# Straight stores of diagonal blocks, grouped norms, stores on another queue and two moved adds in a hybrid encoder layer

## The chip, the cores and the metric

One core of a Trainium2 chip runs the whole program. The metric is the device time of one execution in microseconds (us); less is better. The engines are TensorE (PE, matrix products; PEld is its weight load), VectorE (DVE), ScalarE (ACT), GpSimd (POOL) and SyncE (SP, which here only issues transfers). SP, ACT and GpSimd each have a queue of their own for issuing DMA transfers, and every engine and every queue works through its instructions in the order in which the program has them.

## The reference

One layer over 512 rows of width 2048, all in float32:

```python
h = rmsnorm(x, mix_norm)
proj = h @ w_mix_in
y_gdn = gdn_group(proj, ...)            # 8 heads of 128, gated delta rule
y_sc = shortconv_group(proj, sc_conv)   # gated short convolution, 1024 channels
x = x + concatenate([y_gdn, y_sc]) @ w_mix_out
x = x + memory_xattn(rmsnorm(x), rmsnorm(mem), w_q, w_k, w_v, w_o)   # 4 heads, 256 memory rows
x = x + conv_ffn(rmsnorm(x), w_up, conv_w, w_down)                   # SwiGLU, width 5632
return rmsnorm(x, final_norm)
```

In the delta-rule group, per head and chunk, with k normalised and `beta` and the decay from the projection:

```python
a_strict = where(strict, (k * beta) @ k.T * decay, 0)
sol = triangular_solve(eye + a_strict, [v * beta, k * beta * exp(g)], unit_diagonal=True)
attn = q @ k.T * decay
# over the chunks: v_new = u - w @ state; o = q' @ state + attn @ v_new; state = state * exp(g_last) + k'.T @ v_new
o = rmsnorm(o, out_gain) * silu(z)
```

## The kernel before, in words

**Products.** PE multiplies in a rounded float32 format, so every weight piece (128 x 1024, `wst`) is split in two: ACT casts the high part (`whi`, lines 146 and 516) and DVE subtracts for the low part (`wlo`, lines 147 and 517). A piece is multiplied by 8 products with `whi` over 512 columns and 8 with `wlo` over 256. `wst` has 5 buffers in the delta-rule stage, and SP issues the weights' loads.

**Order of work.** The memory's values come first (`values`, 28 pieces after the early ones; `beside_values(j)` puts other work ahead of piece j: loads of x, the sum of its squares in `xacc`, its norm, x's scaling). Then the folds of w_xv with w_xo, the input projection, the delta-rule stage, the rest of the attention, the FFN and the last norm. In blocks under `tc.manual_schedule` the named engines do their work in the order in which it is written; elsewhere a scheduler orders it.

**Pairs of projection blocks.** The input projection (20 pairs, `quads`) and the FFN's up-projection (44 pairs) multiply two neighbouring 2 x 2 block columns by seven products on sums of blocks. `quad_left` makes products 1, 2, 6 and 5, `quad_right` 7, 3 and 4. Products 1, 6, 7 and 4 share the accumulator `px`, 5 and 3 share `pz`: product 7 can't begin until `gb`, the copy of product 6, has been taken off `px`, nor product 3 until `ub`, the copy of product 5, has been taken off `pz`. For pair 0 the sums of blocks are made beforehand. In pair 1 the tiles `s1` and `s3` are made by two adds after product 2; later pairs get them by another way. `between[0]` to `between[3]` are calls put at set places of `quad_left`. In the FFN `run_held` takes up the unit held back from the pair before: norm of the gate half (`ug`), its convolution (`ucv`), Silu, the same for the up half (`uu`, without Silu), and their product `h`. For pair 1 the norm itself is ended in `between[0]` (`norm_rest`).

**Delta-rule stage.** PE goes through the products of w_xk (`psk`), w_xq (`pswk`) and the out projection in two rounds (`out_row`, `psx`; the second, for the delta rule's own heads, needs `yg`, read back from `y_d`). Chains of small work are woven into them by hand: `weave(chain, wait)` starts a generator, `place(cost)` and `tick` advance a clock by estimated PE time, and what a generator yields is PE's cost of the step and the time until its next one. For each half `hb` (4 heads) and chunk j:

- `prepare_chunk` loads decay, k and q, forms k's squared norms `ss`, the factors `bk` (1/ss times beta) and `nk` (its root, by Ln and Exp on ACT), and the matrix `nt` (128 x 128 for each of 4 heads). It then takes `nt`'s diagonal 32 x 32 blocks: a product with a mask into `nd`, a sum over the four blocks in a row into `ndc`, and a store to `nd_d`.
- `invert` reads the blocks of all four chunks back (`ab`), inverts them on DVE by 31 steps (`tm`, `xb`) and stores the inverses (`xd_d`).
- `solve` reads v and the inverses (`xd`), builds the inverse of the whole chunk (`pt`) and takes `nk`.
- `recur` goes over the chunks in order (`pv`, `vn`, `pso`, `pss`).
- `scaled` takes a result's sum of squares over the head on PE (`psn`), Ln and Exp on ACT, multiplies the result by it on DVE and by z on GpSimd, and stores it to `y_d`.

## Time and profile before

| | |
|---|---|
| median of 3 runs | 2705.7 us (2701.09 to 2709.1) |
| the profiled execution | 2705.68 us, span 2703.9 us, granted clock 0.996 |
| PE busy | 2657.2 us, 98% |
| DVE, ACT, POOL busy | 2261.4 us (84%), 1588.1 us (59%), 217.0 us (8%) |

The profile comes from one execution. A row of PE's waits gives what PE waited for, the total, the number of waits and the longest. A row of a timeline gives the start, the duration (for a group, from its first start to its last end), the engine, the line of the kernel, the operation, the tiles (output, arrow, inputs) and shapes; in brackets the engine's idle time ahead of it and what ended that. A row of a window gives its bounds and length, the busy time of PE, PEld, DVE, ACT and POOL with the number of instructions, then PEclk (the granted clock, 1 is full), the share of DMA time and GB/s. A row of a group of instructions gives minimum, median and maximum in ns, or busy time and mean. A row of DMA issues ends with KB and the median us from issue to landing.

Times by stage: values to about 106 us, first pair of the mixer at about 205 to 225, the delta-rule stage at about 750 to 1125, the FFN's first pairs at about 1400 to 1445.

### The profile page before, as it was taken

The numbers are of one execution on the slowest core, as the hardware profiler recorded it, in microseconds if no ns is written. First come the engines' busy times: TensorE is split into PE (matmuls) and PEld (weight loads), VectorE is DVE, ScalarE is ACT, GpSimd is POOL, SyncE is SP. The second block draws the span as 40 slices with busy tenths as digits, with TensorE's granted clock in tenths as the row PEclk, the third lists the DMA queues.
The fourth block names the chain that finished last, engine by engine and source line by source line (L and its number), as shares of the span: only waits on it lengthen the run. The fifth ranks groups of instructions, "written<-read, shape, count | busy, mean of one in ns | idle before, by whom it ended". The sixth has DMA issues, their size and how long they took to land.

```text
span 2703.9 us, 40155 instructions
## 1 busy us (share of the span) xinstructions
PE 2657.2 (98%) x14757; PEld 2292.9 (85%) x14757; DVE 2261.4 (84%) x3354; ACT 1588.1 (59%) x2305; POOL 217.0 (8%) x236
## 2 busy tenths in 40 slices
PE   9999999999998999999999999999999999999998
PEld 7878888888887897888888888888888888888886
DVE  7868788999999864456688999999999999877888
ACT  7675555666676565345675656565565655554545
POOL 0000000000100123000000000000000000000201
PEclk9999999999999999999999999999999999999999
DMA  8786766776676975665556676777767676864976
GB/s 298 234 259 183 183 162 174 189 199 183 186 222 204 312 226 174 229 199 189 172 171 165 177 192 174 197 182 180 191 178 202 167 198 204 257 189 141 285 248 183
DMA packets 265461, 544.69 MB, mean 201 GB/s; under 512 B 31776, under 2 KB 126640, under 8 KB 265264
## 3 DMA queue, kind: packets, MB, share of 16 engines
q1 hardware_dynamic: 192512, 400.53, 45.4%
q0 software_dynamic: 27920, 89.42, 19.2%
q10 hardware_dynamic: 44832, 52.18, 5.4%
q8 instruction: 115, 1.88, 0.3%
q14 instruction: 82, 0.67, 0.1%
HBM read 472.83 MB, written 67.39 MB: 200 GB/s over the span
## 4 chain that ended last, share of the span: by engine, by line
PE 87%; DVE 5%; DMA 4%; issue 2%; ACT 2%; SPq 0%; POOL 0%; ACTq 0%; DVEq 0%; POOLq 0%
PE px L172 19%; PE px L175 10%; PE pz L172 10%; PE pz L175 5%; PE py L172 5%; PE psd L1487 4%; PE psd L1485 4%; PE psd L1486 4%; PE psx L157 3%; PE psx L159 3%; PE psx L158 3%; PE py L175 2%; PE psk L172 2%; PE psk L1052 2%; PE pss L1145 1%
## 5 line engine op out<-in xcount | busy, mean ns | idle before, releaser
L172 PE MATMUL px<-xo,whi 128*128 128x512 f32 x2288 | 575.7, 394 | 6.7 <-ACT gb L598 5.2
L516 ACT CAST whi<-wst 128x1024 fp32r<-128x1024 f32 x290 | 304.8, 1051 | 343.5 <-PE pz L172 198.7
L172 PEld LDWEIGHTS px<-xo,whi 128*128 128x128 f32 x2288 | 412.8, 189 | 82.2 <-ACT gb L598 5.4
L517 DVE TENSOR_TENSOR wlo<-wst,whi 128x1024 fp32r<-128x1024 f32 x290 | 353.4, 1220 | 22.8 <-ACT whi L516 21.0
L175 PEld LDWEIGHTS px<-xo,wlo 128*128 128x128 f32 x2288 | 312.8, 191 | 22.4
L147 DVE TENSOR_TENSOR wlo<-wst,whi 128x1024 fp32r<-128x1024 f32 x204 | 255.4, 1254 | 90.1 <-ACT whi L146 87.9
L175 PE MATMUL px<-xo,wlo 128*128 128x256 f32 x2288 | 319.6, 283 | 0.0
L516 ACT CAST whi<-s 128x1024 fp32r<-128x1024 f32 x214 | 223.2, 1043 | 158.0 <-DVE wlo L517 83.8
L146 ACT CAST whi<-wst 128x1024 fp32r<-128x1024 f32 x204 | 213.6, 1049 | 165.0 <-issue 48.0
L172 PE MATMUL pz<-xo,whi 128*128 128x512 f32 x1152 | 289.0, 393 | 0.0
L517 DVE TENSOR_TENSOR wlo<-s,whi 128x1024 fp32r<-128x1024 f32 x214 | 261.1, 1221 | 0.2
L1487 PE MATMUL psd<-wlo,hdh 128*128 128x512 f32 x616 | 240.8, 391 | 2.9 <-DVE wlo L1281 2.8
L1485 PE MATMUL psd<-whi,hdh 128*128 128x512 f32 x616 | 240.0, 390 | 0.1
L1486 PE MATMUL psd<-whi,hdl 128*128 128x512 f32 x616 | 239.9, 389 | 0.0
L172 PEld LDWEIGHTS pz<-xo,whi 128*128 128x128 f32 x1152 | 207.2, 189 | 37.1 <-ACT whi L516 0.3
L1278 ACT CAST whi<-wst 128x1024 fp32r<-128x1024 f32 x99 | 104.3, 1053 | 122.6 <-issue 54.1
L175 PEld LDWEIGHTS pz<-xo,wlo 128*128 128x128 f32 x1152 | 157.2, 190 | 11.2
L175 PE MATMUL pz<-xo,wlo 128*128 128x256 f32 x1152 | 160.6, 282 | 0.0
L1487 PEld LDWEIGHTS psd<-wlo,hdh 128*128 128x128 f32 x616 | 115.6, 188 | 30.1 <-DVE wlo L1281 6.2
L172 PE MATMUL py<-xo,whi 128*128 128x512 f32 x560 | 140.2, 392 | 0.0
L1281 DVE TENSOR_TENSOR wlo<-wst,whi 128x1024 fp32r<-128x1024 f32 x99 | 121.2, 1224 | 20.5 <-ACT whi L1278 18.2
L1485 PEld LDWEIGHTS psd<-whi,hdh 128*128 128x128 f32 x616 | 115.6, 188 | 24.2 <-ACT whi L1278 0.4
(368 smaller groups left out, 5045.7 us busy)
## 6 DMA issues: line engine op xcount, KB each, us to landing
wst<-in_w_up SPq DMA_DIRECT2D x132, 512.0 KB, 4.0
wst<-in_w_dn SPq DMA_DIRECT2D x121, 512.0 KB, 4.5
s<-in_w_up POOLq DMA_DIRECT2D x87, 512.0 KB, 6.2
wst<-in_w_mix SPq DMA_DIRECT2D x84, 512.0 KB, 5.5
s<-in_w_mix POOLq DMA_DIRECT2D x55, 512.0 KB, 6.2
s<-in_w_up SPq DMA_DIRECT2D x43, 512.0 KB, 4.4
hid<-hf_d SPq DMA_DIRECT2D x77, 256.0 KB, 5.1
wst<-in_w_xo SPq DMA_DIRECT2D x32, 512.0 KB, 4.7
```

What stands on the lines that cost most here:

```text
L146: nc.scalar.copy(hi, st)
L147: nc.vector.tensor_tensor(lo, st, f(hi), op=ALU.subtract)
L157: nc.tensor.matmul(ps, wh, xh, start=first, stop=False)
L172: nc.tensor.matmul(ps, hi[:, k * P : (k + 1) * P], x, start=first and k == 0, stop=False, skip_group_check=True)
L175: nc.tensor.matmul(ps[:, n:], lo[:, k * P : (k + 1) * P], x[:, :n], start=False, stop=end, skip_group_check=True)
L516: nc.scalar.copy(hi, t)
L517: tt(lo, t, f(hi), op=ALU.subtract)
L1278: nc.scalar.copy(hi[:, i * n : (i + 1) * n], t)
L1281: tt(lo[:, sl], t, f(hi)[:, sl], op=ALU.subtract)
L1485: nc.tensor.matmul(ps, xh, wh, start=first, stop=False)
L1486: nc.tensor.matmul(ps, xl, wh, start=False, stop=False)
L1487: nc.tensor.matmul(ps, xh, wl, start=False, stop=last)
```

## The change

1. In `beside_values` the first norm of x begins at j 12 (was 10), ends at 14, x is scaled at 15 to 26 and the memory's norm taken at 27, each two pieces later.
2. In pair 1 of the mixer and of the FFN the two adds that make `s1` and `s3` are put on DVE behind the add to `ub` of the pair before (`behind`).
3. In the FFN's pair 1 `run_held` is called after `gb`'s copy and no longer ahead of product 6's split.
4. `prepare_chunk` stores the four diagonal blocks of `nt` by four transfers from GpSimd's queue, without the masked product, the sum and SP's store.
5. k's norms of the four chunks of a half lie in one tile of 16 columns; Ln and Exp are taken once for each half, in `invert`.
6. In `scaled` the results of chunks 0 and 1, and of 2 and 3, are finished together: z's load, the Exp and both multiplications of the even chunk wait for the odd one. The stores of `y_d`, and that of `xd_d` in `invert`, are issued by GpSimd.
7. The second half's `prepare_chunk` starts 75 clock units after the first half's (was 60), its `invert` 80 (was 65).

In each fence below, first the line of the kernel, then the operation, output, arrow, inputs, shape. ACT in the FFN's pair 1, from product 1's copy `ga` to product 5's copy `ub`, before:

```order
L577 COPY ga_14073<-px_14056 128x512
L516 CAST whi_14169<-s_2593_14044 128x1024
L516 CAST whi_14192<-wst_14050 128x1024
L1337 ACTIVATE ucv_14104<-ug_14101,cols 128x512
L516 CAST whi_14214<-wst_14048 128x1024
L1351 ACT_TABLE_LOAD
L1351 ACTIVATE ucv_14104<-ucv_14104 128x512
L1337 ACTIVATE ucv_14112<-uu_14109,cols 128x512
L598 COPY gb_14144<-px_14056 128x512
L603 COPY ub_14167<-pz_14146 128x512
```

and after:

```order
L577 COPY ga_14041<-px_14024 128x512
L516 CAST whi_14115<-s_2576_14069 128x1024
L516 CAST whi_14137<-s_2565_14012 128x1024
L534 ACTIVATE s_2603_14222<-wst_14216 128x1024
L516 CAST whi_14160<-wst_14018 128x1024
L599 COPY gb_14094<-px_14024 128x512
L1349 ACTIVATE ucv_14099<-ug_14096,cols 128x512
L516 CAST whi_14182<-wst_14016 128x1024
L1363 ACT_TABLE_LOAD
L1363 ACTIVATE ucv_14099<-ucv_14099 128x512
L1349 ACTIVATE ucv_14107<-uu_14104,cols 128x512
L604 COPY ub_14135<-pz_14114 128x512
```

`gb`'s copy now stands ahead of the held unit's convolution and table load; `ub`'s copy stays behind the whole of it.

DVE in the same place, from the splits of pair 1 to the norm's product `ug` (`rst`, `rsy` are the norm's last steps, `s_2643` a sum for pair 2), before:

```order
L517 TENSOR_TENSOR wlo_14125<-s_2610_14122,whi_14124 128x1024
L517 TENSOR_TENSOR wlo_14148<-s_2609_14119,whi_14147 128x1024
L238 TENSOR_TENSOR rst_13970<-rsy_13969 128x512
L593 TENSOR_TENSOR s_2643_14320<-s_2627_14245,wst_14248 128x1024
L239 SCALAR_TENSOR_TENSOR rst_13970<-rst_13970,ms_13967 128x512
L583 TENSOR_TENSOR ga_14073<-py_14079,ga_14073 128x512
L240 SCALAR_TENSOR_TENSOR rsy_13969<-rst_13970,rsy_13969 128x512
L565 TENSOR_TENSOR ga_14073<-ga_14073 128x256
L1346 TENSOR_TENSOR ug_14101<-ga_13908,rsy_13969 128x256
```

and after:

```order
L238 TENSOR_TENSOR rst_13938<-rsy_13937 128x512
L517 TENSOR_TENSOR wlo_14075<-s_2577_14072,whi_14074 128x1024
L239 SCALAR_TENSOR_TENSOR rst_13938<-rst_13938,ms_13935 128x512
L583 TENSOR_TENSOR ga_14041<-py_14047,ga_14041 128x512
L240 SCALAR_TENSOR_TENSOR rsy_13937<-rst_13938,rsy_13937 128x512
L565 TENSOR_TENSOR ga_14041<-ga_14041 128x256
L517 TENSOR_TENSOR wlo_14116<-s_2576_14069,whi_14115 128x1024
L1358 TENSOR_TENSOR ug_14096<-ga_13876,rsy_13937 128x256
```

The sum for pair 2 has left the place between the norm's steps, and the split of `s1` has come behind `ga`.

SP in the products of w_xq, where the second half's chunks are prepared, before:

```order
L884 DMA nd_d_79<-ndc_8665 128x4x32
L143 DMA wst_8906<-in_w_xq 128x1024
L143 DMA wst_8940<-in_w_xq 128x1024
L143 DMA wst_8984<-in_w_xq 128x1024
L143 DMA wst_9022<-in_w_xq 128x1024
L884 DMA nd_d_79<-ndc_8821 128x4x32
L910 DMA xd_d_80<-xb_8059 128x512
L143 DMA wst_9062<-in_w_xq 128x1024
L895 DMA ab_8840<-nd_d_79 128x1x512
```

and after:

```order
L143 DMA wst_9035<-in_w_xq 128x1024
L840 DMA v_8809<-qkvz_d 128x4x128
L925 DMA xd_8811<-xd_d_80 128x4x32
L143 DMA wst_9069<-in_w_xq 128x1024
L143 DMA wst_9109<-in_w_xq 128x1024
L840 DMA v_8920<-qkvz_d 128x4x128
L925 DMA xd_8922<-xd_d_80 128x4x32
L143 DMA wst_9182<-in_w_xq 128x1024
L900 DMA ab_8966<-nd_d_79 128x1x512
```

The stores of `ndc` and of the inverses have left SP's queue; the reads of `xd` and `ab`, which need GpSimd's stores, are still in it, with weights behind them.

The diff:

```diff
@@ -445,13 +445,13 @@
             squares(2 * j - 1)
         elif 8 < j < 16:
             mem_squares(j - 8)
-        if j == 10:
+        if j == 12:
             r0.append(norm_begin([xacc]))
-        elif j == 12:
+        elif j == 14:
             r0[0] = norm_end(r0[0])
-        elif j > 12 and j < 25:
-            norm_x(j - 13)
-        elif j == 25:
+        elif 14 < j < 27:
+            norm_x(j - 15)
+        elif j == 27:
             mem_cols()
 
     with tc.manual_schedule(engines={mybir.EngineType.PE, mybir.EngineType.SP, mybir.EngineType.Activation, mybir.EngineType.DVE}):
@@ -586,8 +586,9 @@
         if pos == 1:
 
             s1 = US("s1")
-            tt(s1, s3, a22, op=ALU.add)
-            tt(s3, s3, a11, op=ALU.subtract)
+            with tc.issue_after(behind[0].ins):
+                tt(s1, s3, a22, op=ALU.add)
+                tt(s3, s3, a11, op=ALU.subtract)
         if pos:
             s2 = US("s2")
             tt(s2, s1, a11, op=ALU.subtract)
@@ -604,11 +605,13 @@
         between[3]()
         return a12, a22, s2, s3, px, pz, ga, gb, ub
 
+    behind = []
+
     def quad_right(pos, left, whole):
 
         a12, a22, s2, s3, px, pz, ga, gb, ub = left
         product(px, wsplit(s3), 7, False)
-        tt(ub, px, ub, op=ALU.add)
+        behind[:] = [tt(ub, px, ub, op=ALU.add)]
         if not whole:
             together(ub)
         if pos:
@@ -830,7 +833,7 @@
             nc.tensor.transpose(v4(ps)[:, n], v4(t)[:, n], ident)
 
     kx, nt, at, bk, nk, pt, vv, ke, qd, qq = ({} for _ in range(10))
-    prepared, solved = [0, 0], {}
+    prepared, solved, sums = [0, 0], {}, {}
 
     def load4(s2, t, hb, j):
         d = T(s2)
@@ -855,7 +858,9 @@
         turn4(pst, k)
         four(psk, k, k)
         yield 1.4, 2.5, 0
-        ss = sp.tile([P, 4], F32, tag="ss", name=nm("ss"), bufs=3)
+        if j == 0:
+            sums[hb] = sp.tile([P, 16], F32, tag="ss", name=nm("ss"))
+        ss = sums[hb][:, 4 * j : 4 * j + 4]
         junk = T("junk")
         for n in range(4):
             nc.scalar.activation(v4(junk)[:, n], v4(pst)[:, n], AF.Square, accum_out=ss[:, n : n + 1])
@@ -866,9 +871,6 @@
         kx[i] = T("kx")
         nc.vector.tensor_tensor(v4(kx[i]), v4(pst), bc(kd[:, j, H4], P), op=ALU.mult)
         yield 0, 1.5, 0
-        nk[i] = sp.tile([P, 4], F32, tag="nk", name=nm("nk"), bufs=8)
-        nc.scalar.activation(nk[i], ss, AF.Ln, scale=0.25)
-        nc.scalar.activation(nk[i], nk[i], AF.Exp, scale=0.5)
         nt[i] = T("nt")
         for n in range(4):
             nc.vector.scalar_tensor_tensor(v4(nt[i])[:, n], v4(psk)[:, n], bk[i][:, n : n + 1], v4(dt)[:, n], op0=ALU.mult, op1=ALU.mult)
@@ -877,17 +879,20 @@
         four(psq, k, q)
         yield 0.9, 1.5, 0
         nc.vector.tensor_tensor(dt, psq, dt, op=ALU.mult)
-        nd = T("nd")
-        nc.vector.tensor_tensor(v4(nd), v4(nt[i]), mrep(M_BLK), op=ALU.mult)
-        ndc = T("ndc")[:, : 4 * B].rearrange("p (j c) -> p j c", j=4)
-        nc.vector.tensor_reduce(ndc, v4(nd).rearrange("p j (b c) -> p j c b", c=B), axis=AX.X, op=ALU.add)
-        nc.sync.dma_start(nd_d[hb][j].rearrange("n b r c -> (b r) n c"), ndc)
+        for b in range(NB):
+            d = slice(b * B, (b + 1) * B)
+            nc.gpsimd.dma_start(nd_d[hb][j][:, b].rearrange("n r c -> r n c"), v4(nt[i])[d, :, d])
         prepared[hb] += 1
         yield 0, 0, 0
 
     def invert(hb):
         while prepared[hb] < 4:
             yield 0, 1.0, 0
+        n16 = sp.tile([P, 16], F32, tag="nk", name=nm("nk"))
+        nc.scalar.activation(n16, sums[hb], AF.Ln, scale=0.25)
+        nc.scalar.activation(n16, n16, AF.Exp, scale=0.5)
+        for j in range(4):
+            nk[hb, j] = n16[:, 4 * j : 4 * j + 4]
         ab = []
         for i in range(2):
             t = T("ab")
@@ -907,7 +912,7 @@
             nc.vector.tensor_tensor(x[:, :n, m + 1 :], x[:, :n, m + 1 :], t, op=ALU.subtract)
             if m % 2:
                 yield 0, 2.75, 0
-        nc.sync.dma_start(xd_d[hb].rearrange("j n b (g c) r -> (j n b g) c r", g=G), x)
+        nc.gpsimd.dma_start(xd_d[hb].rearrange("j n b (g c) r -> (j n b g) c r", g=G), x)
         for j in range(4):
             weave(solve(hb, j), 4.0 + 8.0 * j)
         weave(recur(hb), 30.0)
@@ -1007,7 +1012,6 @@
         nc.scalar.activation(o, pso, AF.Identity, scale=hgain)
         nc.scalar.activation(q, q, AF.Square, scale=0.128)
         nc.gpsimd.tensor_tensor(s1, s1, q, op=ALU.add)
-        z = load4("z", 3, hb, j)
         yield 0, 4.0, 0
         sh, sl = split(s1, "sn")
         yield 0, 6.0
@@ -1015,20 +1019,28 @@
         nc.tensor.matmul(psn, onesr, sh, start=True, stop=False)
         nc.tensor.matmul(psn, onesr, sl, start=False, stop=True)
         nc.scalar.activation(s1, psn, AF.Ln, bias=cst[:, 1:2], scale=1.0 / P)
-        nc.scalar.activation(s1, s1, AF.Exp, scale=-0.5)
-        yield 0.5, 2.5, 0
-        nc.vector.tensor_tensor(o, o, s1, op=ALU.mult)
-        nc.gpsimd.tensor_tensor(o, o, z, op=ALU.mult)
-        nc.sync.dma_start(y_d[4 * hb : 4 * hb + 4, :, j * P : (j + 1) * P].rearrange("h p c -> p h c"), v4(o))
+        kept[hb, j] = s1, o
+        yield 0.5, 1.0, 0
+        if j % 2 == 0:
+            return
+        for n in (j - 1, j):
+            s1, o = kept.pop((hb, n))
+            z = load4("z", 3, hb, n)
+            nc.scalar.activation(s1, s1, AF.Exp, scale=-0.5)
+            nc.vector.tensor_tensor(o, o, s1, op=ALU.mult)
+            yield 0, 1.2, 0
+            nc.gpsimd.tensor_tensor(o, o, z, op=ALU.mult)
+            nc.gpsimd.dma_start(y_d[4 * hb : 4 * hb + 4, :, n * P : (n + 1) * P].rearrange("h p c -> p h c"), v4(o))
         yield 0, 0
 
+    kept = {}
     order += [g["w_xk"][n, i] for n in range(KT) for i in range(2)]
     order += [g["w_xq"][i, q] for i in range(KT) for q in range(2)]
     order += [g["w_mo"][n, 1] for n in range(KT)]
     for hb in range(2):
         for j in range(4):
-            weave(prepare_chunk(hb, j), 4.0 + 10.0 * j + hb * 60.0)
-        weave(invert(hb), 20.0 + hb * 65.0)
+            weave(prepare_chunk(hb, j), 4.0 + 10.0 * j + hb * 75.0)
+        weave(invert(hb), 20.0 + hb * 80.0)
 
     def loaded(src):
         t = T("yg")
@@ -1408,7 +1420,7 @@
         if i == 1:
             tbs[0].close()
             open_pool(uss, "us", 4, reuse_waits="tile")
-        left = quad_left(i, up_blocks(i) if i else None, first, norm_rest if i == 1 else turn_rest, run_held, first_units if i == NF - 1 else nothing, norm_rows)
+        left = quad_left(i, up_blocks(i) if i else None, first, norm_rest if i == 1 else turn_rest, nothing if i == 1 else run_held, first_units if i == NF - 1 else run_held, norm_rows)
         if i < NF - 1:
             ga, gb, ua, ub = quad_right(i, left, False)
             gate = gate_half(up_order[i], normed(ga, gb, "ug")) if i else (ga, gb)
```

## The prediction

> **What bounds the kernel now.** I read the page's busy times and its chain first, then TensorE's (PE's) waits over the whole span, then the timelines at the places that the change touches.
>
> ```profile
> span 2703.9 us, 40155 instructions
> PE 2657.2 (98%) x14757; PEld 2292.9 (85%) x14757; DVE 2261.4 (84%) x3354; ACT 1588.1 (59%) x2305; POOL 217.0 (8%) x236
> PE 87%; DVE 5%; DMA 4%; issue 2%; ACT 2%; SPq 0%; POOL 0%; ACTq 0%; DVEq 0%; POOLq 0%
> ```
>
> PE is busy 98% of the span and carries 87% of the chain. The change takes no product away, so only PE's idle time, and slow products behind it, can be won; work taken from DVE, ACT or a queue counts where PE waits for it. PE's waits (total, times, longest):
>
> ```profile
> PE px L172 <- ACT gb L598: 5.2, 1, 5.2
> PE pswk L1076 <- DVE wlo L147: 4.5, 6, 1.6
> PE pso L990 <- DVE vn L981: 3.7, 1, 3.7
> PE pskt L830 <- DMA k<-qkvz_d: 3.7, 2, 2.9
> PE psn L255 <- DVE xacc L410: 3.1, 1, 3.1
> PE pswk L1072 <- ACT wk L1079: 1.6, 1, 1.6
> PE px L172 <- DVE ub L611: 1.5, 2, 0.9
> PE pv L826 <- DVE pt L956: 1.3, 1, 1.3
> PE pso L990 <- issue: 1.2, 1, 1.2
> PE psk L1055 <- DVE wlo L147: 1.1, 1, 1.1
> ```
>
> They lie in three places: the first norm (xacc, 3.1 us), the two first pairs (gb 5.2 in the FFN's, ub 1.5 over both) and the delta-rule stage (the other seven rows, 17.1 us). The change touches all three. A wait can cost more than its idle time:
>
> ```profile
> 52.11 1.76 PE L255 MATMUL psn<-xacc,ones 128*128 128x512 f32 x2 [3.05 <-DVE xacc L410]
> 52.88 3.82 PE L172 MATMUL psk<-mw,whi 128*128 128x512 f32 x8
> 52.00:57.00 5.00, 4.89 (x14) 3.38 (x15) 3.64 (x6) 4.47 (x6) 0.15 (x1) 0.66 0.94 269
> 1428.84 2.00 PE L172 MATMUL pz<-xo,whi 128*128 128x512 f32 x8
> 1437.00 3.78 PE L172 MATMUL px<-xo,whi 128*128 128x512 f32 x8 [5.21 <-ACT gb L598]
> 1442.04 2.01 PE L172 MATMUL pz<-xo,whi 128*128 128x512 f32 x8
> 1437.00:1441.00 4.00, 4.00 (x10) 3.23 (x11) 2.13 (x4) 0.62 (x2) 0.08 (x1) 0.50 0.84 224
> 1031.93 0.67 PE L990 MATMUL pso<-dt,vn 128*128 128x128 f32 x2 [3.71 <-DVE vn L981]
> 1031.90:1034.50 2.60, 2.57 (x12) 2.57 (x13) 0.90 (x2) 0.57 (x1) 0.00 (x0) 0.54 0.88 242
> ```
>
> The granted clock (PEclk, third number from a window's end) fell to 0.66, 0.50 and 0.54 of full speed behind the three waits of over 3 us, and eight products took 3.8 us, not 2.0. At 1437 the piece of 16 products runs 5.04 us to 1442.04; the one from 1428.84 needed at most 2.95 (to 1437.00 − 5.21). So the restart costs 2.1 us there. At 52.88 it is (3.82 − 2.00) = 1.8; at 1031.9, 2.6 × 0.46 = 1.2. The Trainium skill ("TensorE: Matmul & The Clock Gate", Part 1) has the clock at half rate after an idle window of about 3.4 us and back after as long; these rows agree in kind, and 3.05 us of idle already sufficed. Were 3.4 us the sharp bound of a single wait, the first norm's restart would not be there to win, and the sum would be 1.5 less.
>
> **The change, part by part.**
>
> *First norm two steps later.* Its sum's last add was done when PE began at 52.11; two weight pieces of 2.8 us later is about 5.5 us after the piece before it, where xacc has been ready for over 2 us. So 3.05 of idle and most of 1.8 of restart go: −4.5; ends −3.0 (PE meets the next weights instead) and −4.9. Scaling x and the memory's norm also move two steps later; their readers come after the last of these steps, at nothing (end +1, in the range).
>
> *Both first pairs: s1 and s3 behind `ub`.* Two adds leave the front of the `ub` that PE waits for: −0.9 in the mixer's, −0.6 in the FFN's (1.5 in all; end 0, if their later place delays another split).
>
> *FFN's first pair: `gb`'s copy ahead of the held unit.*
>
> ```profile
> 1433.94 1.28 ACT L1351 ACT_TABLE_LOAD   x1 [1.18 <-DVE ucv L1339]
> 1436.39 0.56 ACT L598 COPY gb<-px 128x512 f32<-128x512 f32 x1
> 1436.85 0.59 ACT L603 COPY ub<-pz 128x512 f32<-128x512 f32 x1
> 1427.04 1.23 DVE L593 TENSOR_TENSOR s<-s,wst 128x1024 f32<-128x1024 f32 x1 [1.63 <-issue]
> 1428.78 0.69 DVE L583 TENSOR_TENSOR ga<-py,ga 128x512 f32<-128x512 f32 x1
> 1430.65 0.42 DVE L1346 TENSOR_TENSOR ug<-gb,rsy 128x256 f32<-128x256 f32 x1
> ```
>
> `gb` drains a sum finished by about 1429, but stands on ACT behind the unit's convolution, table load and Silu until 1436.95. Moved, it is done by about 1430 and product 7 follows product 5 without a wait: −5.2 and −2.1 of restart. Next late is `ub`'s copy, still behind that unit; product 3 needs it one product later, at 1431.8 + 2.8 = 1434.6, or 1433.7 with the 0.9 or so by which PE arrives sooner there. Today it would be done at 1437.4. But it loses `gb`'s copy ahead of it (0.5), and its chain starts with `ug` on DVE, which in the new order has lost the add of 1.23 us that stood, with 1.63 us of idle, between the norm's steps, and gains one split of 1.2 there: about 2 us sooner, copy done at 1434.9. Residue 1.2, too short for a restart. Together −5.2 − 2.1 + 1.2 − 0.6 = −6.7; ends −7.9 (no residue) and −5.0 (`ug` gains nothing: residue 2.9).
>
> *Prepared chunks without the mask and the reduction.*
>
> ```profile
> L881 DVE TENSOR_TENSOR nd<-nt,mk x8: 684/686/702, 780.9 to 878.4; 128x512 f32<-128x512 f32 x8
> L883 DVE TENSOR_REDUCE ndc<-nd x8: 1044/1102/1126, 782.4 to 880.3; 128x128 f32<-128x512 f32 x8
> 860.00:900.00 40.00, 34.95 (x285) 33.95 (x284) 31.83 (x80) 25.90 (x44) 0.00 (x0) 1.00 0.76 250
> gc_d<-gct POOLq DMA_DIRECT2D x1, 16.0 KB, 2.1
> mem<-in_mem POOLq DMA_DIRECT2D x8, 256.0 KB, 4.1
> c<-x2t_d POOLq DMA_DIRECT2D x8, 256.0 KB, 10.2
> SPq L910 <- DVE xb L907: 6.2, 2, 5.3
> wst<-in_w_mix SPq DMA_DIRECT2D x84, 512.0 KB, 5.5
> ```
>
> DVE loses 8 × (0.69 + 1.10) = 14.3 us at 781 to 881, where it is busy 32 of 40 us and PE waits for its splits (pswk and psk, 5.6 us) and, behind them, wk (1.6). The 32 stores lie on GpSimd, which does nothing there (0.00 busy). The nearest store on that queue, of 16 KB as these are, landed in 2.1 us; the nearest of the size of y and xd, a load, in 4.1; the farthest, 10.2. I take 2 to 4. SP's queue loses 18 transfers, which waited for DVE or GpSimd ahead of weights and k: the loads of k (3.7 us of PE) should come in time.
>
> *Norms in groups.* 12 table loads go (16 activations become 4), 12 × 1.28 = 15.4 us of ACT. ACT is busy 25.9 of 40 us and releases PE there only for wk; inside the term below. In the results, pairing keeps one Ln and one Exp each, and saves nothing.
>
> *hb1's chains 15 units later.* Takes DVE's work out of the pieces in which it is thickest: same term.
>
> Stage: k's loads −3.7; of the 7.2 of splits and wk 60%, −4.3 (the removed 14.3 us exceed them twofold, but only where they stand ahead); half of vn's 3.7 with its restart 1.2, −2.5, since the chain of results ahead of it is cut:
>
> ```profile
> 1027.17 0.69 DVE L1020 TENSOR_TENSOR so<-so,s 128x512 f32<-128x512 f32 x1 [5.07 <-ACT s L1018]
> ```
>
> DVE stood 5.07 us for an Exp here with vn behind it; in pairs, the Exp and its multiplication still follow each other at once, hence half. New waits for the GpSimd stores and the moved chains: +2. Together −8.5; ends +2 (only the new waits) and −18.3 (all 17.1 us and the restart of 1.2).
>
> *The tail.*
>
> ```profile
> 1082.45 0.40 PE L1015 MATMUL psn<-snh,onesr 128*128 128x512 f32 x1
> 1114.07 0.62 ACT L152 CAST yph<-yg 128x512 fp32r<-128x512 f32 x1
> 1123.10 0.39 PE L157 MATMUL psx<-yph,whi 128*128 128x512 f32 x1
> ```
>
> From the last result's norm to the last operand of the second out projection took 31.6 us. In the new order 117 products lie between that norm and the first product of the row that needs it, not 180; the 180 took 41 us (1082.45 to 1123), so 117 cover 27. The 31.6 held idle times, so 0, end +5.
>
> Sum: −4.5 − 0.9 − 6.7 − 8.5 = −20.6 on the profiled run's 2705.68, which is the runs' median (2705.7): **2685**. The terms' lower ends sum to −32.0, the upper ones to 0; half of the way to either gives 2679 to 2695.
>
> **The rivals.**
> (a) *The stage gives back what it gains.* For: each chain of hb1 starts later while its end is fixed by the out rows, and its waits are small and many (pswk six times), the kind that reappear at the next piece. Against: DVE has 14.3 us less to do. With the stage at 0 and `ug` not sooner: −4.5 − 0.9 − 5.0 = −10.4; with the stage at its upper end, +2, −8.4: 2695 to 2697, and with the tail's end up to 2702.
> (b) *The whole stage comes free.* For: its causes are all shortened or moved; against: pt, vn and the unexplained 1.2 hang on chains that the change leaves as they are. −18.3 with the other terms at their middles, −12.1: 2675; with all at their lower ends 2674, and some 2 us less with the stage's waits too short for the rows above.
> (c) *Slower: SP stands behind GpSimd's stores.* SP issues in order, and the reads of nd and xd wait for the stores to land, with weights behind them. Five weight buffers of 2.8 us, less the longest median of a weight load (5.5), cover 8.5 us, so it decides where SP stands longer than that. With the 10.2 landing and the 5.3 that SP has stood for xb already, 15.5 us: 7.0 idle and a restart of 1.2 at each of four places (the reads of nd and xd of each half), +33 against −12.1 elsewhere: 2726. Against: 2.1 and 4.1 landed on the same queue, and two of the places have other loads between. The Trainium skill ("SBUF — State Buffer", the trap of DVE blocking such a DMA) speaks for it: a GpSimd DMA's descriptors can't be written during certain DVE copies, and 0.62 us become 3.1. No row here shows this; by its figure each landing would be 2.5 longer, within the cover, and the sum stays.
>
> **How the numbers follow.** Forecast 0.63, (a) 0.15, (b) 0.15, (c) with other losses 0.07. About 0.3%, 8.1 us, is what a measurement of this kernel can tell, so faster begins below 2697.6: the forecast and (b), and half of (a), 0.85; same is the other half of (a) and some mild loss, 0.10; slower 0.05. From 2672, (b)'s lower end, to 2702, (a)'s upper, leaves under 0.2 out; the likeliest's own range is the 2679 to 2695 above.
>
> **What would show it.** Right: no wait for xacc and none of over 2 us for gb; in the FFN's first pair a wait of 1 to 1.5 us put down to ub's copy or the Silu ahead of it, with the clock at 1.00; DVE 14 us and ACT 15 us less busy; no wait for k; GpSimd's nd stores landing in 2 to 3 us. Wrong: a new row of PE's waits above 3 us in the stage, above all for weights while SP waits for nd or xd; PE idle ahead of the second out projection's row for y; or ub's copy still after 1436.

## The result, and the profile after

The changed kernel takes 2682.14 us (median of 4 runs, 2681.91 to 2688.87), the kernel before, run again beside it, 2706.95 (4 runs): a ratio of 0.9918, 95% interval 0.9895 to 0.994. The profiled execution took 2681.93 us, its span is 2680.1 us, 23.8 less than before; 20.6 were forecast. The page after, first rows, and four of PE's waits (those that the argument needs):

```profile
span 2680.1 us, 40153 instructions
PE 2652.1 (99%) x14757; PEld 2289.4 (85%) x14757; DVE 2244.7 (84%) x3338; ACT 1572.5 (59%) x2281; POOL 236.7 (9%) x278
```

```profile
PE pswk L1088 <- DVE wlo L147: 4.7, 6, 1.5
PE pz L172 <- ACT ub L604: 2.6, 1, 2.6
PE pso L995 <- DVE vn L986: 1.4, 1, 1.4
PE psrm L334 <- DMA macc<-sq: 1.0, 1, 1.0
```

The waits for gb (5.2), xacc (3.1), k (3.7), ub's add (1.5) and wk (1.6) are gone; vn's fell from 3.7 to 1.4. The waits for wlo in the products of w_xq are as they were (4.5 before), and two are new: 2.6 us for `ub`'s copy and 1.0 for `macc`. DVE is 16.7 us less busy, ACT 15.6.

To see where the time went I take the start of the same product in both timelines, at four places: the end of the input projection, the out projection's last rows, the FFN ahead of its pair 0, and a product well behind its pair 1.

| stretch | before | after | difference | forecast |
|---|---|---|---|---|
| start to 740.18 (first norm, mixer's first pair) | 740.18 | 734.76 | −5.4 | −5.4 |
| delta-rule stage, 740.18 to 1150.07 | 409.89 | 398.06 | −11.8 | −8.5 |
| 1150.07 to 1380.07 (attention, out) | 230.00 | 230.02 | 0 | 0 |
| FFN's first pairs, 1380.07 to 1460.18 | 80.11 | 74.66 | −5.5 | −6.7 |
| 1460.18 to the end | 1243.7 | 1242.6 | −1.1 | 0 |

The last row is no part of the change: that stretch, which none of the edits touches, takes 1242.0 to 1245.0 us in the kernels of this study.

**First norm.** PE after:

```profile
53.17 1.12 PE L175 MATMUL psk<-mw,wlo 128*128 128x256 f32 x8
54.12 1.02 PE L255 MATMUL psn<-xacc,ones 128*128 128x512 f32 x2
98.03 1.02 PE L334 MATMUL psrm<-ones,macc 128*128 128x1 f32 x8 [0.99 <-DMA macc<-sq]
```

`psn` follows its predecessor without a wait, and the clock stays up. That gave 5.3 us; 1.0 of it went back where PE, now earlier, met the last of the memory's squares, which GpSimd adds up by transfers. Of the nine kernels below with the same work up to here, two have this wait at `psrm` (0.8 and 0.9 us) and seven don't.

**FFN's first pair.** ACT, DVE and PE after, from the norm's step `rst` to product 3:

```profile
1411.64 0.58 ACT L599 COPY gb<-px 128x512 f32<-128x512 f32 x1
1416.19 1.28 ACT L1363 ACT_TABLE_LOAD   x1 [1.17 <-DVE ucv L1351]
1418.63 0.56 ACT L604 COPY ub<-pz 128x512 f32<-128x512 f32 x1
1407.55 0.68 DVE L238 TENSOR_TENSOR rst<-rsy 128x512 f32<-128x512 f32 x1
1408.15 1.22 DVE L517 TENSOR_TENSOR wlo<-s,whi 128x1024 fp32r<-128x1024 f32 x1
1409.89 0.68 DVE L583 TENSOR_TENSOR ga<-py,ga 128x512 f32<-128x512 f32 x1
1411.43 1.22 DVE L517 TENSOR_TENSOR wlo<-s,whi 128x1024 fp32r<-128x1024 f32 x1
1412.90 0.42 DVE L1358 TENSOR_TENSOR ug<-gb,rsy 128x256 f32<-128x256 f32 x1
1413.74 2.00 PE L172 MATMUL px<-xo,whi 128*128 128x512 f32 x8
1419.25 2.11 PE L172 MATMUL pz<-xo,whi 128*128 128x512 f32 x8 [2.55 <-ACT ub L604]
```

Product 7 (1413.74) meets `gb` ready. Product 3 then waits 2.55 us for `ub`'s copy, which stands behind the table load and Silu; 1.2 were forecast. `ug` is done at 1413.3, only 0.5 us sooner than before once the 17.2 us by which everything is earlier here are taken off (1431.07 before). DVE has no idle time on the way. `rst` begins when it did before (1407.55; 1424.72 before, less the 17.2), and two splits of 1.22 us (1408.15 and 1411.43) now stand between it and `ug`, where the sum for pair 2 and 1.63 us of idle time stood. Both splits stood ahead of `rst` before; the adds of `s1` and `s3`, which the change puts behind the add to `ub`, have come in their stead.

**Stage.** SP and the GpSimd stores (issue to landing), then DVE's longest wait for the inverses of the first half, before (the first chunk's) and after (the third chunk's, with SP's issue of the read ahead of it):

```profile
SPq L900 <- DMA nd_d<-nt: 4.2, 4, 3.0
SPq L925 <- DMA xd_d<-xb: 1.6, 1, 1.6
y_d<-so POOLq DMA_DIRECT2D x8, 256.0 KB, 5.5
nd_d<-nt POOLq DMA_DIRECT2D x32, 16.0 KB, 3.6
xd_d<-xb POOLq DMA_DIRECT2D x2, 256.0 KB, 3.5
```

```profile
893.74 0.69 DVE L925 TENSOR_TENSOR pt<-xd,mk 128x512 f32<-128x512 f32 x1 [4.33 <-DMA xd<-xd_d]
```

```profile
886.60 0.50 SPq L925 DMA_DIRECT2D xd<-xd_d  x1
894.80 0.69 DVE L930 TENSOR_TENSOR pt<-xd,mk 128x512 f32<-128x512 f32 x1 [7.14 <-DMA xd<-xd_d]
895.74 1.22 DVE L147 TENSOR_TENSOR wlo<-wst,whi 128x1024 fp32r<-128x1024 f32 x1
897.01 0.39 PE L1088 MATMUL pswk<-kth,wlo 128*128 128x256 f32 x1 [0.87 <-DVE wlo L147]
```

SP stands up to 3.0 us for a GpSimd store, far from the 8.5 at which, by the prediction's estimate, it would reach PE. But DVE, too, works in order: at 894.80 it has stood 7.14 us for `xd`, with a split of weights behind it, and PE waits for that split. What is late is the read itself. SP issued it at 886.60 and it landed 8.2 us later, the slowest of the eight reads of `xd`; the store that it needs had been issued 17.9 us before it, at 868.70. SP's 4.2 us for `nd` come just ahead of this read and may have held it; no run parts that from the rest.

### The profile page after: what moved, and what is told of

The parts are those of the page before. It is cut to its first block, busy times and chain, and to the rows that moved or that the text cites. A ratio compares the mean times of both kernels' runs of the same rounds, so it can differ in the third digit from the quotient of the medians.

```text
span 2680.1 us, 40153 instructions
## 1 busy us (share of the span) xinstructions
PE 2652.1 (99%) x14757; PEld 2289.4 (85%) x14757; DVE 2244.7 (84%) x3338; ACT 1572.5 (59%) x2281; POOL 236.7 (9%) x278
## 4 chain that ended last, share of the span: by engine, by line
PE 58%; DVE 3%; DMA 1%; ACT 1%; issue 1%; SPq 0%; ACTq 0%; DVEq 0%
PE px L172 12%; PE px L175 6%; PE pz L172 6%; PE psd L1499 4%; PE psd L1497 4%; PE psd L1498 4%; PE psx L157 3%; PE psx L158 3%; PE psx L159 3%; PE pz L175 3%; PE py L172 3%; PE py L175 1%; PE pss L1157 1%; PE pss L1158 1%; PE pss L1159 1%
## 5 line engine op out<-in xcount | busy, mean ns | idle before, releaser
L1293 DVE TENSOR_TENSOR wlo<-wst,whi 128x1024 fp32r<-128x1024 f32 x99 | 121.0, 1222 | 18.7 <-ACT whi L1290 16.3
L1498 PEld LDWEIGHTS psd<-whi,hdl 128*128 128x128 f32 x616 | 115.6, 188 | 24.1
```

Of the source, the lines that this page charges most:

```text
L1293: tt(lo[:, sl], t, f(hi)[:, sl], op=ALU.subtract)
L1498: nc.tensor.matmul(ps, xl, wh, start=False, stop=False)
```

## The experiments

Times from separate rounds are each compared with the kernel before, run beside them, and most intervals of the single edits overlap the changed kernel's. The stage's length from the profiles separates them better, within limits: three kernels that don't differ in the stage (the changed one, e5 and e6) give 398.06, 398.43 and 398.25 us, but e10 and e11, which don't differ there either, give 395.77 and 398.46. Most of those 2.7 us arise behind a single wait, where the granted clock fell in one profile and not in the other (the last section has the numbers). So a difference of less than 3 us between two stages shows nothing.

| kernel | median us | ratio to before (95%) | stage us | PE's waits there |
|---|---|---|---|---|
| changed | 2682.14 | 0.9918 (0.9895 to 0.994) | 398.06 | 7.4 |
| e1: mask, sum, SP store again | 2688.86 | 0.9935 (0.992 to 0.995) | 403.82 | 12.3 |
| e2: second half at 60 and 65 again | 2683.7 | 0.9914 (0.9899 to 0.9929) | 398.99 | 9.6 |
| e3: y_d, xd_d on SP again | 2680.32 | 0.9904 (0.9889 to 0.9918) | 393.48 | 6.5 |
| e4: k's norms one by one again | 2688.36 | 0.9936 (0.9919 to 0.9952) | 404.41 | 10.8 |
| e7: before, straight stores alone | 2700.22 | 0.9982 (0.9972 to 0.9991) | 404.69 | 12.2 |
| e8: changed, pt 6 units later | 2674.28 | 0.9882 (0.9866 to 0.9899) | 389.75 | 3.2 |
| e9: e8 with e4's norms | 2679.93 | 0.9908 (0.9893 to 0.9923) | 397.43 | 8.5 |
| e10: e8 with e3's stores | 2681.13 | 0.9908 (0.9893 to 0.9923) | 395.77 | 8.0 |
| e11: e10 with three more edits, outside the stage | 2677.87 | 0.9894 (0.9878 to 0.9911) | 398.46 | 8.5 |
| e12: before, pt 6 units later | 2703.43 | 0.9996 (0.9986 to 1.0005) | 409.75 | 17.9 |

**e1, diagonal blocks as before.**

```diff
-        for b in range(NB):
-            nc.gpsimd.dma_start(nd_d[hb][j][:, b]..., v4(nt[i])[d, :, d])
...
+        nc.vector.tensor_tensor(v4(nd), v4(nt[i]), mrep(M_BLK), op=ALU.mult)
...
+        nc.vector.tensor_reduce(ndc, ...)
+        nc.sync.dma_start(nd_d[hb][j].rearrange("n b r c -> (b r) n c"), ndc)
```

> The changed kernel with the diagonal blocks taken as before: masked product, sum over the blocks and one store on SP for each chunk; all else as changed. If DVE's load in the delta-rule stage and the stores that held SP are what was won there (theory A), 14.3 us of DVE come back between 780 and 900 us, PE's waits in the stage rise from 7.5 us to 13 or more and the kernel is 6 to 10 us slower than the changed one, some 2690. If the later start of the second half's chains won it (theory B), PE's waits in the stage stay below 9.5 us and the time within 2 us of the changed kernel's 2682.

The stage is 5.8 us longer and the waits for wlo 9.0 us, not 4.7:

```profile
PE pswk L1090 <- DVE wlo L147: 9.0, 3, 4.2
```

All waits of the stage, 12.3 us, stay a little below theory A's 13, its time holds; B is out. DVE's arithmetic and SP's stores come back together here, so their shares are not told apart.

**e2, the second half's chains as early as before.**

```diff
-            weave(prepare_chunk(hb, j), 4.0 + 10.0 * j + hb * 75.0)
-        weave(invert(hb), 20.0 + hb * 80.0)
+            weave(prepare_chunk(hb, j), 4.0 + 10.0 * j + hb * 60.0)
+        weave(invert(hb), 20.0 + hb * 65.0)
```

> The changed kernel with the second half's chains at 60 and 65 clock units, as before. Theory A (DVE's load and SP's stores): PE's waits in the stage rise by at most 3 us, the time to 2685 at most. Theory B (the later start): they rise by 6 us or more, the time to 2688 to 2694.

The time is theory A's, the waits rise by 2.2 us, and B is out. The 0.9 us of stage are too few to tell from nothing: what the later start alone is worth lies within the spread.

**e3, stores of results and inverses on SP again.**

```diff
-        nc.gpsimd.dma_start(xd_d[hb]..., x)
+        nc.sync.dma_start(xd_d[hb]..., x)
...
-            nc.gpsimd.dma_start(y_d[...], v4(o))
+            nc.sync.dma_start(y_d[...], v4(o))
```

> The changed kernel with the stores of the results (y_d) and of the inverses (xd_d) on SP's queue as before; the diagonal blocks stay on GpSimd. Theory A as I hold it: SP stands for the results again (44.6 us over 8 stores before), but the weights' buffers cover it: within 1.5 us of the changed kernel. Theory C (SP's queue in order was the brake): 4 us or more slower, with PE waiting for weights or for k.

Neither: the time is 1.8 us less than the changed kernel's, where theory A had at most 1.5 either way and theory C 4 more, and the stage is 4.6 us shorter. Most of that is the clock's doing. Both kernels have a wait of 1.4 us for a split ahead of the same product (854.7 and 855.5). Behind it the granted clock fell in the changed kernel and stayed up here; the changed kernel first, then e3:

```profile
840.00:860.00 20.00, 18.18 (x128) 17.19 (x127) 18.07 (x53) 9.71 (x29) 2.18 (x4) 0.91 0.70 219
840.00:860.00 20.00, 18.34 (x138) 17.15 (x138) 17.59 (x51) 10.64 (x29) 2.17 (x4) 1.00 0.70 218
```

At 920 to 940 it fell once more in the changed kernel (0.92, shown with e8) and not here (1.00). Between the same products e3 gains 1.5 us at each of the two places, 3 of its 4.6. The rest is within the spread, so this run shows no gain from the move of these stores to GpSimd, and no sure loss. DVE's longest wait for `xd` is 5.3 us here against 7.1, but not because the inverses land sooner: their two stores took 4.0 us in the median from SP and 3.5 from GpSimd.

**e4, k's norms one by one again.** In `prepare_chunk`, with `invert`'s lines on `n16` taken out:

```diff
-        ss = sums[hb][:, 4 * j : 4 * j + 4]
+        ss = sp.tile([P, 4], F32, tag="ss", name=nm("ss"), bufs=3)
...
+        nc.scalar.activation(nk[i], ss, AF.Ln, scale=0.25)
+        nc.scalar.activation(nk[i], nk[i], AF.Exp, scale=0.5)
```

> The changed kernel with k's norms taken for each chunk as before, 12 table loads and 12 activations more on ACT (about 15.4 us and more of ACT). Theories A and B: PE waits for ACT in the stage only once and for 1.6 us, so 0 to 2 us slower. Rival D (ACT's table loads delayed the casts that DVE's splits wait for): 4 us or more slower, with the waits for wlo risen from 4.7 us to 8 or more.

6.3 us of stage, against an expectation of at most 2. ACT shows a way. With single norms, then with grouped ones, behind the squares of one chunk:

```profile
847.80 1.28 ACT L873 ACT_TABLE_LOAD   x1
849.09 0.20 ACT L873 ACTIVATE nk<-ss 128x4 f32<-128x4 f32 x1
849.21 1.03 ACT L146 CAST whi<-wst 128x1024 fp32r<-128x1024 f32 x1
850.26 1.28 ACT L874 ACT_TABLE_LOAD   x1
851.55 0.20 ACT L874 ACTIVATE nk<-nk 128x4 f32<-128x4 f32 x1
851.66 0.35 ACT L341 COPY kt<-psk 128x256 f32<-128x256 f32 x1
```

```profile
847.17 1.06 ACT L146 CAST whi<-wst 128x1024 fp32r<-128x1024 f32 x1
848.11 0.40 ACT L341 COPY kt<-psk 128x256 f32<-128x256 f32 x1
```

Counted from the chunk's squares (the first begins at 846.64, and at 846.16 with grouped norms), a cast and a copy from which PE's operands are made come 1.6 and 3.1 us later, behind one table load and behind two. That ACT is idle 41% of the span does not help them. Rival D's time holds; its number for the waits (8 or more for wlo) was missed, with 6.0 for wlo and 1.0 for `kth`. In all the waits rise by 3.4 us, and the granted clock stands at half for 17 us of the stage, against 7 in the changed kernel.

**e5, the two adds of pair 1 not ordered.**

```diff
-            with tc.issue_after(behind[0].ins):
-                tt(s1, s3, a22, op=ALU.add)
-                tt(s3, s3, a11, op=ALU.subtract)
+            tt(s1, s3, a22, op=ALU.add)
+            tt(s3, s3, a11, op=ALU.subtract)
```

> The changed kernel without the order for the two adds of pair 1 (s1 and s3 again ahead of ub's add). Theory E: those adds, put behind ub, now fill the idle time that DVE had ahead of the norm's steps, so that the held unit and with it ub's copy come no sooner; without them there the wait of product 3 for ub's copy falls from 2.5 us to 1 or less in the FFN's first pair, while the waits for ub's add come back (0.9 in the mixer's, 0.6 in the FFN's). Sum between -2 and +1 us against the changed kernel. Rival F: the wait for ub's copy is set by ACT's table load and Silu alone and stays at 2.5 us; then 1.5 to 2.5 us slower.

2685.5 us, 0.9929 (0.9915 to 0.9944). The wait for ub's copy is 2.54 us as in the changed kernel, and waits for ub's add are back, 1.25 us in the mixer's pair and 0.93 in the FFN's. Theory E falls. Rival F holds in its number, and the loss of 3.4 us is 1 more than it gave. But F's reason is not shown either. In this kernel DVE's place is taken by the sum for pair 2 again:

```profile
1410.76 1.22 DVE L593 TENSOR_TENSOR s<-s,wst 128x1024 f32<-128x1024 f32 x1 [0.62 <-DVE rst L238]
1412.50 0.68 DVE L583 TENSOR_TENSOR ga<-py,ga 128x512 f32<-128x512 f32 x1
1415.51 0.42 DVE L1357 TENSOR_TENSOR ug<-gb,rsy 128x256 f32<-128x256 f32 x1
```

`ga`'s add of product 2 comes 1.7 to 1.8 us after that product's end in both (PE's next product starts at 1410.77 here and at 1408.05 after the change), and `ug` follows it at the same distance, 3.01 us. That fits a chain to `ub`'s copy that hangs on product 2 and moves with PE. It is argued from two profiles: in both DVE has a piece of work of 1.22 us and a step of the norm ahead of that add, the sum for pair 2 here and a split there. In the profiles 1.5 us of the difference are the restart behind that wait, which came here and not in the changed kernel (last section).

**e6, the held unit in two parts**, called for pair 1 in `between[2]` and, behind ub's copy, in `between[3]`:

```diff
+    def held_gate():
+        pos, ua, ub, (a, b) = held_up.pop()
+        cv = unit_conv(normed(a, b, "ug"), up_order[pos])
+        half[:] = [pos, normed(ua, ub, "uu"), cv]
+    def held_rest():
+        pos, uu, cv = half
+        nc.scalar.activation(cv, cv, AF.Silu)
+        up_half(pos, uu, cv)
```

> The changed kernel with the held unit of the FFN's pair 1 cut in two: norm and gate convolution after gb's copy as now, Silu with its table load, the up half's convolution and the product only after ub's copy. Theory E: product 3's wait of 2.54 us goes, and with it the restart at half clock (1.5 us where it came): 2.5 to 4 us faster than the changed kernel, 2678 to 2680. Rival G: the next wait takes its place (DVE's sums of ub and gb behind the later up half), less than 1 us faster.

2682.83 us, 0.992 (0.9905 to 0.9935): no gain, as rival G has it, though not by the wait that it named. Product 3 does not wait; product 6 of pair 2 does, for the split of its sum, which DVE reaches after the held unit's later work and the next unit's:

```profile
1427.78 1.21 DVE L594 TENSOR_TENSOR s<-s,wst 128x1024 f32<-128x1024 f32 x1
1430.12 3.50 PE L172 MATMUL px<-xo,whi 128*128 128x512 f32 x8 [2.35 <-ACT whi L516]
```

**e7, the kernel before with straight stores alone** (e1's edit the other way round, in the kernel before).

> The kernel before with one part of the change alone: the diagonal blocks stored straight from nt by GpSimd, without mask, sum and SP's store. Theory A: DVE has 14.3 us less to do and SP eight stores less ahead of k's loads: PE's waits in the stage fall from 18.7 us to 12 or less, the time by 5 to 8 us to some 2700. Theory B (it pays only with the chains of the second half later): waits above 16 us, time within 2.5 us of before.

The stage is 5.2 us shorter, nearly what e1 lost. That is theory A's way, by less than its numbers: the waits come to 12.2 us, not to 12 or less, and the time is 4.3 us below the kernel before beside it, not 5 to 8. B's numbers (waits above 16, within 2.5 us) are farther off. The waits for k are gone, while splits are still late:

```profile
PE pswk L1074 <- DVE wlo L147: 4.3, 1, 4.3
PE psk L1053 <- DVE wlo L147: 3.2, 1, 3.2
```

**e8, the inverses taken later.**

```diff
         nc.sync.dma_start(xd, xd_d[hb][j].rearrange("n b c r -> (b c) n r"))
-        yield 0, 5.0, 0
+        yield 0, 11.0, 0
...
-        yield 0, 8.0
+        yield 0, 2.0
```

> The changed kernel with the step that takes the inverses (pt from xd) placed 6 clock units later and the next step 6 sooner after it. Theory H: DVE stands up to 7.1 us for xd with splits of weights queued behind it, and PE's waits for wlo at 897 and 911 (2.4 us) come from that: DVE's wait for xd falls below 3 us, PE's waits in the stage from 7.5 to 5 us, 2 to 3 us faster than the changed kernel. Rival: the splits are late for another reason (DVE's own work, casts) and PE's waits stay at 7 us or more.

The fastest kernel of this study: its four runs, 2672.1 to 2674.8, lie below all four of the changed one. The stage is 8.3 us shorter, more than forecast: 4.2 us fewer waits, and the granted clock fell at one place and not at two. Some 6 of the 8.3 us arise between 895 and 926, behind DVE's old wait. DVE takes the third chunk's `pt` without a wait, and a split goes ahead of it:

```profile
889.45 1.22 DVE L147 TENSOR_TENSOR wlo<-wst,whi 128x1024 fp32r<-128x1024 f32 x1
897.53 0.68 DVE L930 TENSOR_TENSOR pt<-xd,mk 128x512 f32<-128x512 f32 x1
900.00:920.00 20.00, 20.00 (x237) 19.10 (x236) 18.16 (x35) 13.82 (x24) 4.80 (x4) 1.00 1.01 310
920.00:940.00 20.00, 18.75 (x199) 17.84 (x199) 19.40 (x43) 12.66 (x21) 5.30 (x5) 1.00 0.76 246
```

The same windows of the changed kernel have PE 17.14 and 18.61 us busy, and a granted clock of 0.92 in the second:

```profile
900.00:920.00 20.00, 17.14 (x224) 15.86 (x223) 19.19 (x36) 11.74 (x20) 3.96 (x3) 1.00 1.02 320
920.00:940.00 20.00, 18.61 (x191) 17.87 (x188) 18.95 (x35) 9.97 (x17) 7.05 (x5) 0.92 0.71 234
```

**e9, e8 with single norms** (both edits as above).

> The changed kernel with both the norms of k taken for each chunk (as in the run on single norms, 6.2 us slower than the changed kernel) and the inverses taken 6 units later (as in the run on late pt, 7.9 us faster). Theory H (what ACT's extra work cost went through DVE, which stood for xd with splits behind it): with that wait gone single norms cost 2 us or less, so 2677 at most. Rival D (ACT's 12 table loads and activations hold the casts directly): they cost 5 us or more here too, 2679 to 2681.

5.7 us slower than e8 (stage 7.7): the loads and activations cost without DVE's wait for `xd`, which is gone here too, as with it. Rival D; my theory that their price went through DVE's wait falls.

**e10, e8 with e3's stores** (both edits as above).

> The run on late pt with the stores of results and inverses back on SP. If these stores cost on GpSimd because xd lands later (theory H), little is left of the 1.8 us that they gained alone: within 1.5 us of 2674.3. If GpSimd's queue costs by itself (later results, rival C'), 3 us or more are gained, 2671 or less.

Missed by both: 6.9 us slower. Up to the last out rows it is 1.8 us ahead of e8 (0.7 of it from ahead of the stage, and 1.7 from the place near 855, where the clock fell in e8 and not here), and then loses more at one place, the second out projection's row for y:

```profile
PE psx L157 <- ACT yph L152: 4.1, 1, 4.1
```

```profile
1099.31 0.32 SPq L1098 DMA_DIRECT2D xp_d<-x0r  x1
1100.87 0.38 SPq L1047 DMA_DIRECT2D yg<-y_d  x1
```

The last read of `yg` is issued at 1100.87, behind the store of an out row, for whose sum SP stood 6.1 us. With the results stored by GpSimd (e8) the last such read is issued at 1093.95, and PE doesn't wait. The last result was not later here: its store is issued at 1082.00, and at 1082.25 in e8. That leaves the place of the read in SP's order, in which SP also stands for the results (up to 9.0 us at a time); no run tried it by itself.

**e11, all together**: e10 with e6's two parts and

```diff
             a11, a12, a22, s1, s3 = pair_loads(blocks, pos)
+            if pos == 2:
+                s2 = US("s2")
+                tt(s2, s1, a11, op=ALU.subtract)
...
-        elif 8 < j < 16:
-            mem_squares(j - 8)
+        if 6 < j < 14:
+            mem_squares(j - 6)
```

> The run on late pt with these added: stores of results and inverses on SP; the FFN's held unit of pair 1 cut in two and pair 2's sum for product 6 made first; the sum of squares of the memory begun two pieces sooner. Theory E': the wait of 2.54 us for ub's copy, the 2.35 us that took its place in the run on the split unit, and a restart of up to 1.5 us go, and the 1.0 us wait of psrm for macc: 4 to 5 us faster than the run on late pt, 2669 to 2671. Rival G: in the FFN's first pairs DVE is full (it had no idle time from product 2 on), and another wait of 2 us comes at pair 2 or 3: 2672 to 2675.

2677.87 us, 0.9894 (0.9878 to 0.9911), slower than e8 and outside the numbers of both. It has e10's wait at the tail (3.6 us). The FFN's first pairs, over the stretch of the table above, take 72.66 us, against 76.16 in e8 and 74.66 in the changed kernel, with waits of 0.7 and 0.4 us left: theory E' holds there, with 3.5 us. A version of e8 with only this part was not run.

**e12, the kernel before with pt later** (e8's edit).

> The kernel before with only the inverses taken 6 clock units later. Theory H': in the kernel before DVE stood 5.8 us for xd too, but PE's waits there came mostly from DVE's own work, k's loads and vn: 0 to 4 us faster, PE's waits in the stage 15 us or more. Rival: the wait for xd was what held the whole stage: 8 us or more faster.

No difference that can be measured, within theory H', and a stage as long as before: there `pt` in its later place makes PE itself wait (5.4 us for `pt` at the transpose), and k's loads and the splits hold as ever. The edit that gives 8 us after the change gives nothing ahead of it.

## Why the forecast came out as it did

*First norm and mixer's pair: right.* −5.4 as summed, though that it is the same to a tenth is chance: the product at the end of this stretch starts at 737.7 to 740.2 us in the three kernels with the old order here and at 733.2 to 735.7 in the nine with the new, medians 4.9 apart. The term "at nothing" for the steps moved along was not nothing: 1.0 us at `psrm`, within its end of +1.

*FFN's first pair: right way, one step wrong.* `gb`'s wait and its restart went as forecast. The step that failed is "about 2 us sooner". I took off the add for pair 2 and the idle time ahead of it and counted one split in their place; the same change put two there, since its adds for pair 1 stand where the splits stood. `ug` came 0.5 us sooner, `ub`'s copy 1.0: it ended at 1419.19, or 1436.4 in the times of before, which is one of the signs of being wrong that I had named. The residue was 2.55 us and not 1.2. e5 shows that the other order of those adds brings the same 2.54. "Too short for a restart" failed with it: six of the seven other kernels with this order had the restart, and their stretch is 76.2 us, −3.9, outside the term's ends of −7.9 and −5.0. That the profiled −5.5 lies inside is luck.

*The stage: −11.8, not −8.5.* Nearly all of it is waits, 18.7 us before and 7.4 after. Undone one by one, direct stores are worth 5 to 6 us (e1, e7) and grouped norms 6 to 8 (e4, e9); the later chains (0.9, e2) and GpSimd's stores of results and inverses (e3) are not told from nothing. Waits are shared, so these need not add up to 11.8. The norms were the term I mis-sized most: I had put them "inside the term below", since ACT released PE only once, and the runs show 6 us or more for them; the order on ACT (e4) is how I explain it. Of the splits' and wk's 7.2 us, wk and the one in w_xk went (2.7), but not those in w_xq, at 4.7. The wait for `pt` at `pv` and the "issue", which I had left standing, went; 0.8 us for `pt` at another product stays. vn's wait fell by 2.3 us, close to the half that I gave it, but not shown to be for my reason: e3 and e4 keep the results in pairs and have 3.0 and 2.9 us for vn, and no run undid the pairing.

*Rival (c) saw the stores and not the waiter.* GpSimd's stores did land later than the nearest rows said (3.6 us for `nd`, 5.5 for `y`; 2.1 and 4.1 expected), and SP's standing for them reached PE nowhere that the trace shows. It was DVE that stood, for the read of `xd`, a wait that was there before (4.33) and that I had not costed. That the later stores lengthened it is not shown: it is 8.4 us in e1, where SP stores the blocks again, and 5.3 in e3, where SP stores the inverses. The Trainium skill's trap ("SBUF — State Buffer") was the rule that I weighed for (c); the longest landing of a store of `nd` or `xd` in the changed kernel was 6.8 us, below the 10.2 that would have decided, and none of these runs separates DVE's part in it.

*The tail: right here.* No wait came, but e10 and e11 show the term at 3.6 to 4.1 us and a restart.

*The total.* 2682.1 against 2685: the stage gave 3.3 us more than its term and the FFN's pair 1.2 less, 1.1 came from a stretch that the change does not touch, and 1.5 of the FFN's is luck. So the way was right, the terms less than the sum suggests.

## What to carry to other kernels

On an engine that works in order, ask what stands behind each instruction, not how busy the engine is: twelve table loads and activations ahead of casts cost about as much (e4, 6.3 us of stage) as 14 us of arithmetic and eight stores on another queue (e1, 5.8). A step that consumes a transfer belongs behind its landing, above all on the engine that also makes the matrix engine's operands: one step moved by 6 units in a hand-made plan gave 8 us here, and nothing in the kernel in which other waits came first. When an instruction is moved away from a chain, look at what the same edit puts in its place.

## What the runs showed of the hardware that I had not expected

The same idle time does not always cost a restart. Nine kernels had the wait of 2.54 or 2.55 us for ub's copy at the same products. In seven the 16 products behind it took 4.1 to 4.4 us, in two (the changed kernel and e9) 2.90. Windows of 4 us from the wait's end, the changed kernel first, then e2:

```profile
1419.25:1423.25 4.00, 4.00 (x21) 3.49 (x22) 4.00 (x8) 1.95 (x2) 0.30 (x1) 1.00 0.92 366
1419.18:1423.18 4.00, 4.00 (x13) 3.28 (x14) 3.46 (x6) 1.22 (x2) 0.18 (x1) 0.58 0.90 362
```

The granted clock was 1.00 in one and 0.58 in the other behind the same wait. The stage shows the same with a shorter wait: nine kernels have one of 1.43 or 1.44 us ahead of the same product near 855. Behind it the 40 next products took 4.8 us in four of them (e3, e5, e6, e10) and 6.2 to 7.5 in five (the changed kernel, e4, e8, e9, e11), with the clock at half for at least 3.4 us. So a single profile tells such a place to 1.5 us at best, and the changed kernel's pair in the FFN was a lucky one: in six of the seven others with its order the stretch of the table is 1.5 us longer. The Trainium skill ("TensorE: Matmul & The Clock Gate", Part 1) has the activity counted in windows that run free of the program, which would let the same wait fall differently; that fits, but its window of about 3.4 us of idle is longer than the 2.54 and the 1.43 that sufficed here.
